# Transposing DMAs of one plane of a block, or of both planes together, in place of four small ones, in a two-layer decoder trunk

## The chip, the cores and the metric

The kernel runs on one core of one Trainium2 chip. The metric is the device time of one execution in microseconds. The time before is 2111.49 us, the median of three runs (2111.09 to 2111.51).

## The reference

Two pre-norm residual layers over 256 rows of 2048 columns in float32. The first mixes with sliding-window attention and an mLSTM, the second with forgetting attention; each is followed by a SwiGLU FFN with 5632 hidden columns.

```python
def swiglu(xn, w_gate, w_up, w_down):
    return (jax.nn.silu(xn @ w_gate) * (xn @ w_up)) @ w_down

    h = x
    for layer in range(DEPTH):
        j = layer // 2
        xn = rms_norm(h, norm_mix[layer])
        if layer % 2 == 0:
            mix = swa_mlstm_mixer(xn, w_in_even[j], w_out_even[j], ...)
        else:
            mix = forgetting_attention_mixer(xn, w_in_odd[j], fox_b_f[j], w_out_odd[j])
        h = h + mix.astype(h.dtype)
        h = h + swiglu(rms_norm(h, norm_ffn[layer]), w_gate[layer], w_up[layer], w_down[layer])
    return rms_norm(h, norm_final)
```

## The kernel before

**Matmuls.** Every float32 operand is split into a high and a low part: ScalarE (ACT) casts to `hi`, VectorE (DVE) subtracts to `lo`, and TensorE (PE) makes three products per tile (`hi` by `hi`, `lo` by `hi`, `hi` by `lo`; lines 184 to 186 and 394 to 396). The activations are kept transposed, 16 column blocks of 128 partitions by 256 rows, in `xh`/`xl` (the normed stream) and `mh`/`ml` (the mixer's outputs, later the FFN's hidden columns). The weights are streamed: `load_raw` (line 112) issues one DMA of 512 KB on SyncE's queue (SP) for each 256 rows by 512 columns, `split_chunk` (lines 156, 157) splits it. Four `raw` buffers and six `hi`/`lo` pairs lie between the load and the matmul; where `pair_group` multiplies two blocks by a scheme with fewer products (`prod`, `ht`/`lt`, `sx`, `sd`), DVE and ACT have more to do per weight block.

**Turned blocks.** A result of a matmul has rows on partitions; as the left operand of the next it must be transposed. For most blocks of 512 columns (both halves of 128 rows, that is 256 by 512 float32) this is done by DMA, which transposes 16-bit elements only. So a block is cut into two *planes*, the low and the high 16 bits of each number:

1. ACT copies each plane into `flat` (128 partitions; two planes of 1024 elements: `t` 0 and 1, 512 columns each): line 235 for the stream `h`, line 587 for FFN blocks.
2. SP issues one transposing DMA for each plane and each half `t`, four in all, each of 128 by 512 elements, into `turned` (lines 241 and 589).
3. `join`: ACT copies each plane of `turned` back to its place among the 16-bit halves of `ct` (lines 246 and 594; one copy reads 1024 elements in a row and writes every second one), and the result is scaled and split into `xh`/`xl` (lines 251, 252) or split into `mh`/`ml` (lines 271, 272); DVE also makes sums of it (`sums_of`, lines 224 to 227) for the scheme with fewer products.

`turn_scaled` does this for the residual stream behind an output projection or the last part of a FFN, 12 blocks in all (four after the first mixer, four between the layers, four after the second mixer). For even `n` its `flat` lies in the tile `c` and its planes are two tiles `turned`; for odd `n` three tiles named `turn` hold the flat planes, the turned planes and the joined block. The FFN's loop turns 20 more blocks of hidden columns (ten per layer), always through `c` and `turned`; the last hidden block of a part goes through TensorE instead.

**Order.** The program is written in the order of the code, and `issue_after` ties a turn's start to a weight load and a join to a cast; within that, a planner sets the order of the instructions on every engine from its own estimate of their times. SP takes its queue in order: a DMA behind another is issued when that one has been, and a DMA whose buffer or source is not ready holds what is behind it. ACT and DVE take their work in order too.

Of the kernel before, what the change touches and what calls it, by code (L numbers as in the profile page):

```python
# [10 lines left out]
U16 = mybir.dt.uint16  # L11
# [6 lines left out]
P = 128  # L18
D = 2048
S = 256  # L20
NT = S // P
KT = D // P
FF = 5632
NB = 512
# [35 lines left out]
def trunk(  # L60
# [20 lines left out]
    nc = tc.nc  # L81
# [137 lines left out]
    def sums_of(room, sh, sl, copies, full=None):  # L219
# [7 lines left out]
        nc.vector.tensor_tensor(out=s[:, 3, :], in0=full[:, 1, 0, :], in1=s[:, 1, :], op=ALU.subtract)  # L227
        split_plain(sh, sl, s)

    def turn_scaled(room, idx, n, extra=None):  # L230

        hu = h[:, :, n * NB : (n + 1) * NB].bitcast(U16).rearrange("p t (n b) -> p t n b", b=2)
        flat, turned, ct = room.turn_tiles(n % 2)
        for b in range(2):
            nc.scalar.copy(flat[:, b, :, :], hu[:, :, :, b])

        def start():
            with tc.issue_after(load[0].ins):
                for b in range(2):
                    for t in range(NT):  # L240
                        nc.sync.dma_start_transpose(turned[b][:, :, t, :], flat[:, b, t, :])

        def join():
            cb = ct.bitcast(U16).rearrange("p (n b) -> p n b", b=2)
            for b in range(2):
                nc.scalar.copy(cb[:, :, b], turned[b].rearrange("p k t q -> p (k t q)"))
            cols = ct.rearrange("p (k q) -> p k q", k=4)
            for i in range(4):
                k = 4 * n + i
                g = gT[:, idx * KT + k : idx * KT + k + 1]  # L250
                nc.scalar.mul(xh[:, k, :], cols[:, i, :], g)
                nc.vector.scalar_tensor_tensor(
                    out=xl[:, k, :], in0=cols[:, i, :], scalar=g, in1=xh[:, k, :].bitcast(F32), op0=ALU.mult, op1=ALU.subtract
                )
            for half in range(2):
                pair = 2 * n + half
                if extra is None or pair not in mixed_of(ORDER):
                    continue
                m = mixed_of(ORDER).index(pair)

                def copies(full, half=half, pair=pair):
                    for i in range(2):
                        g = gT[:, idx * KT + 2 * pair + i : idx * KT + 2 * pair + i + 1]
# [137 lines left out]
    class Room:  # L401
# [23 lines left out]
            return self.pool.tile(shape, F32, tag="tmp", name=name, bufs=2)  # L425

        def turn_tiles(self, odd):
            shape = [P, 4, NT, P]
            if odd:
                a, b, ct = (self.pool.tile([P, 2 * NB], F32, tag="raw", name="turn", bufs=self.raws) for _ in range(3))  # L430
                flat = a.bitcast(U16).rearrange("p (b t n) -> p b t n", b=2, t=NT)
                turned = [
                    b.bitcast(U16)[:, i * 2 * NB : (i + 1) * 2 * NB].rearrange("p (k t q) -> p k t q", k=4, t=NT)
                    for i in range(2)
                ]
                return flat, turned, ct
            c = self.c()
            flat = (
                c[:, 2:4, :].bitcast(U16).rearrange("p a n -> p (a n)").rearrange("p (b t n) -> p b t n", b=2, t=NT)
            )  # L440
            turned = [self.pool.tile(shape, U16, tag="tmp", name="turned", bufs=2) for _ in range(2)]
            return flat, turned, c[:, 0:2, :].rearrange("p a n -> p (a n)")

    class Inside(Room):
# [93 lines left out]
    def ffn(layer, fp, room, pending, sx, sd, key, idx_next=None, key_next=None, finish=None, then=None):  # L538
# [6 lines left out]
        for g0, g1 in zip(PARTS, PARTS[1:]):  # L545
# [5 lines left out]
            for g in range(g0, g1):  # L551
                par = (g1 - 1 - g) % 2
                plain, c = pair_group(
                    room, par, x_of, sums_x, [(w_gate[layer], g * NB), (w_up[layer], g * NB)], ORDER, todo
                )
                todo = []
                for m in range(2):
                    for t in range(NT):
                        o = c[:, 2 * m + t, :]
                        nc.vector.tensor_tensor(out=o, in0=plain[m][t], in1=o, op=ALU.add)  # L560
                for t in range(NT):
                    nc.scalar.activation(c[:, t, :], c[:, t, :], AF.Silu, scale=r[:, t : t + 1])
                for t in range(NT):
                    nc.vector.scalar_tensor_tensor(
                        out=c[:, t, :], in0=c[:, 2 + t, :], scalar=r[:, t : t + 1], in1=c[:, t, :], op0=ALU.mult, op1=ALU.mult
                    )
                if g == g1 - 1 and nk < 16:
                    for half in range(2):
                        pt = bank(par, "pf").rearrange("p (i q) -> p i q", i=2)
                        for i in range(2):  # L570
                            cs = (2 * half + i) * P
                            for t in range(NT):
                                nc.tensor.transpose(pt[:, i, t * P : (t + 1) * P], c[:, t, cs : cs + P], ident)
                        pair = 2 * (g - g0) + half
                        k = 2 * pair
                        split_plain(mh[:, k : k + 2, :], ml[:, k : k + 2, :], pt)
                        if pair in mixed_of(order):
                            j = mixed_of(order).index(pair)
                            sums_of(
                                room, sd[0][:, j, :, :], sd[1][:, j, :, :], lambda full, pt=pt: nc.scalar.copy(full, pt)  # L580
                            )
                    continue
                cu = c.bitcast(U16).rearrange("p a (n b) -> p a n b", b=2)
                flat = c[:, 2:4, :].bitcast(U16).rearrange("p a n -> p (a n)").rearrange("p (b t n) -> p b t n", b=2, t=NT)
                turned = [fp.tile([P, 4, NT, P], U16, tag="tmp", name="turned") for _ in range(2)]
                for b in range(2):
                    nc.scalar.copy(flat[:, b, :, :], cu[:, 0:2, :, b])
                    for t in range(NT):
                        nc.sync.dma_start_transpose(turned[b][:, :, t, :], flat[:, b, t, :])
                def join(c=c, turned=turned, g=g, g0=g0, order=order):  # L590
                    ct = c[:, 0:2, :].rearrange("p a n -> p (a n)")
                    cb = ct.bitcast(U16).rearrange("p (n b) -> p n b", b=2)
                    for b in range(2):
                        nc.scalar.copy(cb[:, :, b], turned[b].rearrange("p k t q -> p (k t q)"))
# [15 lines left out]

                todo = [(MID if g < g1 - 1 else MID_DOWN, join)]
# [17 lines left out]
            for n0 in (0, 2):  # L629
                if end and idx_next is None and n0 == 2:  # L630
# [68 lines left out]
    with tc.tile_pool(name="ev", bufs=1) as ev:  # L699
# [156 lines left out]
        with tc.tile_pool(name="mp", bufs=1) as mp:  # L856
# [31 lines left out]
            plain, c = pair_group(room, 0, x_of, sums_m, [(wi, OFF_QM), (wi, OFF_KM)], QK_ORDER)  # L888
# [79 lines left out]
            plain, c = pair_group(room, 0, x_of, sums_m, [(wi, OFF_VM), (wi, OFF_VM + NB)], QK_ORDER)  # L968
# [51 lines left out]
    with tc.tile_pool(name="od", bufs=1) as od:  # L1020
# [62 lines left out]
        for i in range(4):  # L1083
# [141 lines left out]
```

## Time and profile before

| | |
|---|---|
| median of three runs | 2111.49 us |
| the profiled execution | 2111.74 us |
| its span (first to last instruction) | 2110.0 us |
| mean granted TensorE clock | 0.998 |
| PE, DVE, ACT busy | 99%, 86%, 63% of the span |
| transposing DMAs | 128: 80 on line 589, 48 on line 241 |
| weight and input loads on SP, 512 KB | 4.4 to 4.9 us from issue to landing in the median, by matrix |

PE, DVE, ACT and POOL are the engines' busy times; PEld is TensorE's load of the stationary operand, which overlaps PE. SPq stands for SP's issuing instructions: their durations are the time that SP is held by one issue, not the transfer. In the waits, `A <- B: us, times, longest` says that A was idle until B was done. A row of windows gives, for a stretch, the busy time of each engine and in brackets the number of instructions, then the granted clock, the share of DMA time and the GB/s.

### The profile page before, as it was taken

What the parts mean: (1) busy time and instruction counts of PE and PEld (TensorE: products, weight loads), DVE (VectorE), ACT (ScalarE), POOL (GpSimd) and SP (SyncE); (2) the same over time, 40 slices, a digit from 0 to 9 for tenths busy, and PEclk for the clock granted to TensorE, in tenths of its full rate; (3) what the DMA queues carried; (4) which work ended last, traced back from release to release, by engine and by line L of the source; (5) the groups of instructions that cost most, each with busy time, mean ns of one, the idle gap of its engine ahead of it and who ended that gap; (6) DMA issues with size and microseconds to landing.
All of it is one profiled execution on the core that took longest, in us unless ns stands there. A gap on an engine that the chain in (4) does not pass through costs nothing.

```text
span 2110.0 us, 26911 instructions
## 1 busy us (share of the span) xinstructions
PE 2088.3 (99%) x9558; PEld 1729.4 (82%) x9558; DVE 1817.7 (86%) x2402; ACT 1326.3 (63%) x1685; POOL 51.3 (2%) x74
## 2 busy tenths in 40 slices
PE   8999999999999999999999999999999999999998
PEld 6878888888888888888888888887888888888886
DVE  6688757998999999998788878669989999998985
ACT  6575568665577656667765555586755677556763
POOL 2101000000000000000000000000000000000000
PEclk9999999999999999999999999999999999999999
DMA  9446677756677657766685655576756667657763
GB/s 321 120 140 191 218 191 218 251 189 201 191 222 232 210 196 223 210 209 170 197 244 185 186 177 173 167 219 227 237 173 222 221 210 207 219 192 213 228 198 139
DMA packets 285111, 429.35 MB, mean 203 GB/s; under 512 B 82688, under 2 KB 90928, under 8 KB 284976
## 3 DMA queue, kind: packets, MB, share of 16 engines
q1 hardware_dynamic: 283088, 421.79, 64.2%
q0 software_dynamic: 1744, 5.81, 0.9%
q8 instruction: 75, 1.23, 0.2%
q14 instruction: 60, 0.49, 0.1%
q10 hardware_dynamic: 144, 0.03, 0.0%
HBM read 408.67 MB, written 2.11 MB: 195 GB/s over the span
## 4 chain that ended last, share of the span: by engine, by line
PE 82%; DVE 8%; DMA 4%; ACT 3%; issue 2%; SPq 0%; POOLq 0%; POOL 0%; ACTq 0%; DVEq 0%
PE acc L395 17%; PE acc L396 17%; PE acc L394 17%; PE prod L395 4%; PE prod L394 4%; PE prod L396 4%; PE acc L186 4%; PE acc L185 4%; PE acc L184 4%; DVE lo L157 3%; DMA raw<-in_w_up_dram 1%; ACT hi L156 1%; DVE lt L272 1%; PE vacc L186 1%; PE vacc L184 1%
## 5 line engine op out<-in xcount | busy, mean ns | idle before, releaser
L156 ACT CAST hi<-raw 128x1024 fp32r<-128x1024 f32 (+1 forms) x664 | 675.3, 1030 | 431.5 <-PE acc L396 201.1
L157 DVE TENSOR_TENSOR lo<-raw,hi 128x1024 fp32r<-128x1024 f32 (+1 forms) x664 | 786.7, 1199 | 137.6 <-ACT hi L156 135.5
L395 PE MATMUL acc<-lo,xh 128*128 128x512 f32 x1207 | 471.2, 390 | 1.8 <-DVE lo L157 1.8
L396 PE MATMUL acc<-hi,xl 128*128 128x512 f32 x1207 | 467.2, 390 | 0.0
L394 PE MATMUL acc<-hi,xh 128*128 128x512 f32 x1207 | 464.8, 391 | 0.5 <-DVE c L533 0.4
L395 PEld LDWEIGHTS acc<-lo,xh 128*128 128x128 f32 x1207 | 226.8, 188 | 50.5 <-DVE lo L157 4.0
L394 PEld LDWEIGHTS acc<-hi,xh 128*128 128x128 f32 x1207 | 226.6, 188 | 49.3 <-DVE c L533 1.2
L396 PEld LDWEIGHTS acc<-hi,xl 128*128 128x128 f32 x1207 | 226.8, 188 | 46.8
L395 PE MATMUL acc<-lo,mh 128*128 128x512 f32 x444 | 173.1, 390 | 0.0
L396 PE MATMUL acc<-hi,ml 128*128 128x512 f32 x444 | 170.6, 390 | 0.0
L394 PE MATMUL acc<-hi,mh 128*128 128x512 f32 x444 | 169.7, 390 | 0.2 <-ACT hi L156 0.2
L271 ACT CAST ht<-raw 128x1024 fp32r<-128x1024 f32 x94 | 98.7, 1050 | 63.7 <-PE acc L396 29.6
L271 ACT CAST hi<-raw 128x512 fp32r<-128x512 f32 (+1 forms) x115 | 72.4, 630 | 86.1 <-PE acc L396 67.3
L271 ACT CAST ht<-t 128x1024 fp32r<-128x1024 f32 x94 | 98.8, 1051 | 43.8 <-PE prod L396 36.5
L184 PE MATMUL acc<-hi,mh 128*128 128x512 f32 x320 | 126.3, 396 | 0.0
L272 DVE TENSOR_TENSOR lt<-raw,ht 128x1024 fp32r<-128x1024 f32 x94 | 114.9, 1223 | 12.4 <-ACT ht L271 12.2
L185 PE MATMUL acc<-lo,mh 128*128 128x512 f32 x320 | 125.2, 391 | 0.0
L186 PE MATMUL acc<-hi,ml 128*128 128x512 f32 x320 | 124.9, 392 | 0.0
L272 DVE TENSOR_TENSOR lt<-t,ht 128x1024 fp32r<-128x1024 f32 x94 | 114.8, 1221 | 0.3 <-ACT ht L271 0.2
L394 PEld LDWEIGHTS acc<-hi,mh 128*128 128x128 f32 x444 | 83.4, 188 | 17.9 <-ACT hi L156 0.7
L395 PEld LDWEIGHTS acc<-lo,mh 128*128 128x128 f32 x444 | 83.4, 188 | 17.8 <-DVE lo L157 0.5
L396 PEld LDWEIGHTS acc<-hi,ml 128*128 128x128 f32 x444 | 83.4, 188 | 17.0
(387 smaller groups left out, 3554.1 us busy)
## 6 DMA issues: line engine op xcount, KB each, us to landing
raw<-in_w_gate_dram SPq DMA_DIRECT2D x176, 512.0 KB, 4.6
raw<-in_w_up_dram SPq DMA_DIRECT2D x176, 512.0 KB, 4.7
raw<-in_w_down_dram SPq DMA_DIRECT2D x176, 512.0 KB, 4.9
raw<-in_w_in_odd_dram SPq DMA_DIRECT2D x88, 512.0 KB, 4.4
raw<-in_w_in_even_dram SPq DMA_DIRECT2D x64, 512.0 KB, 4.6
raw<-in_w_out_even_dram SPq DMA_DIRECT2D x32, 512.0 KB, 4.4
raw<-in_w_out_odd_dram SPq DMA_DIRECT2D x32, 512.0 KB, 4.7
raw<-in_w_in_odd_dram SPq DMA_DIRECT2D x8, 272.0 KB, 5.0
```

What stands on the lines that cost most here:

```text
L156: latest[0] = nc.scalar.copy(hi[:, :, 0:n], raw[:, :, 0:n])
L157: nc.vector.tensor_tensor(out=lo[:, :, 0:n], in0=raw[:, :, 0:n], in1=hi[:, :, 0:n].bitcast(F32), op=ALU.subtract)
L184: nc.tensor.matmul(o, ah[:, ts], hi, start=(k == 0), stop=False)
L185: nc.tensor.matmul(o, ah[:, ts], lo, start=False, stop=False)
L186: nc.tensor.matmul(o, al[:, ts], hi, start=False, stop=(k == k_all - 1))
L271: nc.scalar.copy(dst_h, src)
L272: nc.vector.tensor_tensor(out=dst_l, in0=src, in1=dst_h.bitcast(F32), op=ALU.subtract)
L394: nc.tensor.matmul(o, ah, hi, start=start, stop=False)
L395: nc.tensor.matmul(o, ah, lo, start=False, stop=False)
L396: nc.tensor.matmul(o, al, hi, start=False, stop=stop)
```

## The change

The planes of `flat` are no longer addressed by half, and a plane of 128 by 1024 elements is transposed by one DMA into `turned` with 8 blocks of 128. Where both planes of the target lie in one tile (the `turn` tiles of odd `n`), one DMA transposes both, 128 by 2048 elements into 16 blocks. In the result the half `t` is now the outer index and the column block `k` the inner one, so the join's copy reads its 1024 elements as 8 runs of 128 in another order (`k`, then `t`). In the FFN loop both flat copies now stand ahead of the DMAs in the code. Counts: 20 FFN blocks and 6 scaled ones with two DMAs each, 6 scaled ones with one: 58 in place of 128. Bytes, copies and matmuls stay.

```diff
+    def turn_planes(turned, flat):
+        if len(turned) == 1:
+            nc.sync.dma_start_transpose(turned[0], flat.rearrange("p b n -> p (b n)"))
+            return
+        for b in range(2):
+            nc.sync.dma_start_transpose(turned[b], flat[:, b, :])
+
+    def join_planes(cb, turned):
+        for b in range(2):
+            one = turned[b] if len(turned) == 2 else turned[0][:, 8 * b : 8 * b + 8, :]
+            nc.scalar.copy(
+                cb[:, :, b].rearrange("p (k t q) -> p k t q", k=4, t=NT), one.rearrange("p (t k) q -> p k t q", t=NT)
+            )
+
     def turn_scaled(room, idx, n, extra=None):
...
         for b in range(2):
-            nc.scalar.copy(flat[:, b, :, :], hu[:, :, :, b])
+            nc.scalar.copy(flat[:, b, :].rearrange("p (t n) -> p t n", t=NT), hu[:, :, :, b])
 
         def start():
             with tc.issue_after(load[0].ins):
-                for b in range(2):
-                    for t in range(NT):
-                        nc.sync.dma_start_transpose(turned[b][:, :, t, :], flat[:, b, t, :])
+                turn_planes(turned, flat)
 
         def join():
             cb = ct.bitcast(U16).rearrange("p (n b) -> p n b", b=2)
-            for b in range(2):
-                nc.scalar.copy(cb[:, :, b], turned[b].rearrange("p k t q -> p (k t q)"))
+            join_planes(cb, turned)
...
         def turn_tiles(self, odd):
-            shape = [P, 4, NT, P]
             if odd:
...
-                flat = a.bitcast(U16).rearrange("p (b t n) -> p b t n", b=2, t=NT)
-                turned = [
-                    b.bitcast(U16)[:, i * 2 * NB : (i + 1) * 2 * NB].rearrange("p (k t q) -> p k t q", k=4, t=NT)
-                    for i in range(2)
-                ]
+                flat = a.bitcast(U16).rearrange("p (b n) -> p b n", b=2)
+                turned = [b.bitcast(U16).rearrange("p (i q) -> p i q", q=P)]
                 return flat, turned, ct
...
-            turned = [self.pool.tile(shape, U16, tag="tmp", name="turned", bufs=2) for _ in range(2)]
+            turned = [self.pool.tile([P, 8, P], U16, tag="tmp", name="turned", bufs=2) for _ in range(2)]
...
-                turned = [fp.tile([P, 4, NT, P], U16, tag="tmp", name="turned") for _ in range(2)]
+                turned = [fp.tile([P, 8, P], U16, tag="tmp", name="turned") for _ in range(2)]
                 for b in range(2):
-                    nc.scalar.copy(flat[:, b, :, :], cu[:, 0:2, :, b])
-                    for t in range(NT):
-                        nc.sync.dma_start_transpose(turned[b][:, :, t, :], flat[:, b, t, :])
+                    nc.scalar.copy(flat[:, b, :].rearrange("p (t n) -> p t n", t=NT), cu[:, 0:2, :, b])
+                turn_planes(turned, flat)
...
-                    for b in range(2):
-                        nc.scalar.copy(cb[:, :, b], turned[b].rearrange("p k t q -> p (k t q)"))
+                    join_planes(cb, turned)
```

The planner sets the order anew. On SP, at the joint of the two layers, where the last blocks of the first layer's stream are turned between the loads of its FFN's last weights and those of the second layer (`w_in_odd`), the queue before was:

```order
L241 DMA_TRANSPOSE turned<-c 128x4x128 x4
L241 DMA_TRANSPOSE turn<-turn 128x4x128 x4
L112 DMA raw<-in_w_down_dram 128x2x512 x6
L112 DMA raw<-in_w_in_odd_dram 128x2x512 x4
L112 DMA raw<-in_w_in_odd_dram 128x2x272 x4
L112 DMA raw<-in_w_in_odd_dram 128x2x512 x2
L241 DMA_TRANSPOSE turned<-c 128x4x128 x4
L241 DMA_TRANSPOSE turn<-turn 128x4x128 x4
L112 DMA raw<-in_w_in_odd_dram 128x2x512 x2
```

and is now, with lines 235 and 232 for the DMA of one plane and of both:

```order
L235 DMA_TRANSPOSE turned<-c 128x8x128 x2
L232 DMA_TRANSPOSE turn<-turn 128x16x128
L112 DMA raw<-in_w_down_dram 128x2x512 x6
L112 DMA raw<-in_w_in_odd_dram 128x2x512 x4
L112 DMA raw<-in_w_in_odd_dram 128x2x272 x4
L112 DMA raw<-in_w_in_odd_dram 128x2x512 x2
L235 DMA_TRANSPOSE turned<-c 128x8x128 x2
L112 DMA raw<-in_w_in_odd_dram 128x2x512 x2
L232 DMA_TRANSPOSE turn<-turn 128x16x128
L112 DMA raw<-in_w_in_odd_dram 128x2x272 x4
```

Two weight loads moved ahead of the last block's transpose; elsewhere on SP the places of the transposes among the loads are the same, or differ by one or two loads.

On ACT, in a FFN block of the first layer (`c<-c` are the flat copies, `c<-turned` the joins, `hi` and `ht` casts of weights, `mh` the cast of the joined block), the rows before were:

```order
L587 COPY c<-c 128x1024 x2
L156 COPY hi<-raw 128x1024 x2
L271 COPY ht<-t_6325 128x1024
L594 COPY c<-turned 128x1024
L271 COPY ht<-raw 128x1024
L594 COPY c<-turned 128x1024
L156 COPY hi<-raw 128x1024
L271 COPY mh<-c 128x1024
```

and are now:

```order
L592 COPY c<-c 128x1024 x2
L156 COPY hi<-raw 128x1024 x2
L282 COPY ht<-t_6303 128x1024
L240 COPY c<-turned 128x1024 x2
L282 COPY ht<-raw 128x1024
L282 COPY mh<-c 128x1024
L156 COPY hi<-raw 128x1024
```

The two joins stand together and the block's cast one weight cast earlier. In 14 of the 20 FFN blocks the two joins stood together before as well.

More of the change, by code (lines that the diff above doesn't have):

```diff
@@ L427, in turn_tiles @@
         def turn_tiles(self, odd):
-            shape = [P, 4, NT, P]
             if odd:
                 a, b, ct = (self.pool.tile([P, 2 * NB], F32, tag="raw", name="turn", bufs=self.raws) for _ in range(3))
-                flat = a.bitcast(U16).rearrange("p (b t n) -> p b t n", b=2, t=NT)
-                turned = [
-                    b.bitcast(U16)[:, i * 2 * NB : (i + 1) * 2 * NB].rearrange("p (k t q) -> p k t q", k=4, t=NT)
-                    for i in range(2)
-                ]
+                flat = a.bitcast(U16).rearrange("p (b n) -> p b n", b=2)
+                turned = [b.bitcast(U16).rearrange("p (i q) -> p i q", q=P)]
                 return flat, turned, ct
             c = self.c()
-            flat = (
-                c[:, 2:4, :].bitcast(U16).rearrange("p a n -> p (a n)").rearrange("p (b t n) -> p b t n", b=2, t=NT)
-            )
-            turned = [self.pool.tile(shape, U16, tag="tmp", name="turned", bufs=2) for _ in range(2)]
+            flat = c[:, 2:4, :].bitcast(U16).rearrange("p a n -> p (a n)").rearrange("p (b n) -> p b n", b=2)
+            turned = [self.pool.tile([P, 8, P], U16, tag="tmp", name="turned", bufs=2) for _ in range(2)]
             return flat, turned, c[:, 0:2, :].rearrange("p a n -> p (a n)")
@@ L583, in ffn @@
                 cu = c.bitcast(U16).rearrange("p a (n b) -> p a n b", b=2)
-                flat = c[:, 2:4, :].bitcast(U16).rearrange("p a n -> p (a n)").rearrange("p (b t n) -> p b t n", b=2, t=NT)
-                turned = [fp.tile([P, 4, NT, P], U16, tag="tmp", name="turned") for _ in range(2)]
+                flat = c[:, 2:4, :].bitcast(U16).rearrange("p a n -> p (a n)").rearrange("p (b n) -> p b n", b=2)
+                turned = [fp.tile([P, 8, P], U16, tag="tmp", name="turned") for _ in range(2)]
                 for b in range(2):
-                    nc.scalar.copy(flat[:, b, :, :], cu[:, 0:2, :, b])
-                    for t in range(NT):
-                        nc.sync.dma_start_transpose(turned[b][:, :, t, :], flat[:, b, t, :])
+                    nc.scalar.copy(flat[:, b, :].rearrange("p (t n) -> p t n", t=NT), cu[:, 0:2, :, b])
+                turn_planes(turned, flat)
                 def join(c=c, turned=turned, g=g, g0=g0, order=order):
```

## The prediction

> **What bounds the kernel now.** I read the page's busy table first, then the windows, to see where TensorE is not fed, and last the waits and the chain in those places.
>
> ```profile
> span 2110.0 us, 26911 instructions
> PE 2088.3 (99%) x9558; PEld 1729.4 (82%) x9558; DVE 1817.7 (86%) x2402; ACT 1326.3 (63%) x1685; POOL 51.3 (2%) x74
> ```
>
> TensorE is the bound: idle for 2110.0 - 2088.3 = 21.7 us. No change to transposing DMAs removes a matmul, so the gain is limited by idle time. Whole windows say where it lies (columns: window, PE, PEld, DVE, ACT and POOL busy with instruction counts, granted clock, DMA share, GB/s).
>
> ```profile
> 0.00:20.00 20.00, 12.63 (x43) 8.96 (x44) 11.11 (x21) 12.94 (x23) 3.51 (x14) 1.00 0.90 289
> 450.00:500.00 50.00, 49.45 (x222) 40.63 (x222) 44.46 (x59) 28.56 (x35) 0.00 (x0) 1.00 0.66 226
> 550.00:600.00 50.00, 50.00 (x222) 41.42 (x222) 45.98 (x55) 33.68 (x36) 0.00 (x0) 1.00 0.73 222
> 2100.00:2110.00 10.00, 1.44 (x7) 0.86 (x5) 3.04 (x6) 2.87 (x4) 0.55 (x1) 0.81 0.53 210
> ```
>
> The first 20 us hold 7.4 us of the idle time (the first loads) and the last 10 us hold 8.6 (the final norm and the store). Neither has a transposing DMA. That leaves 5.7 us. An ordinary FFN window, 550 to 600, has none at all, although a block is turned in it (the first of these two, SP's timeline):
>
> ```profile
> 585.59 5.13 SPq L589 DMA_TRANSPOSE turned<-c  x4
> 590.83 1.89 SPq L112 DMA_DIRECT2D raw<-in_w_gate_dram  x1
> ...
> 624.67 5.19 SPq L589 DMA_TRANSPOSE turned<-c  x4
> ```
>
> Narrow windows at the places near turned blocks where PE is idle:
>
> ```profile
> 1016.00:1020.00 4.00, 3.76 (x17) 2.80 (x16) 4.00 (x8) 4.00 (x7) 0.00 (x0) 1.00 0.55 157
> 1044.00:1048.00 4.00, 3.06 (x18) 2.56 (x18) 2.38 (x5) 4.00 (x7) 0.00 (x0) 1.00 0.59 108
> 1050.00:1054.00 4.00, 3.88 (x18) 2.75 (x17) 2.54 (x5) 3.63 (x7) 0.00 (x0) 1.00 0.62 213
> 1064.00:1068.00 4.00, 3.29 (x16) 2.44 (x16) 4.00 (x9) 3.09 (x5) 0.00 (x0) 1.00 0.77 219
> 1076.00:1080.00 4.00, 3.84 (x17) 2.88 (x16) 3.57 (x7) 3.56 (x6) 0.00 (x0) 1.00 0.45 131
> 380.00:384.00 4.00, 3.60 (x16) 2.47 (x15) 4.00 (x5) 1.05 (x1) 0.00 (x0) 1.00 0.81 260
> 1428.00:1430.00 2.00, 1.94 (x9) 1.29 (x8) 0.92 (x1) 1.05 (x1) 0.00 (x0) 1.00 1.04 381
> 1452.00:1456.00 4.00, 3.04 (x12) 1.88 (x11) 4.00 (x5) 1.05 (x1) 0.00 (x0) 1.00 0.83 268
> sum 30.00, PE 26.40 PEld 19.07 DVE 25.41 ACT 21.43 POOL 0.00; mean PE 3.30 PEld 2.38 DVE 3.18 ACT 2.68 POOL 0.00
> ```
>
> Together 30.00 - 26.40 = 3.6 us: 2.2 at the joint of the two layers (1016 to 1080) and 1.4 in the two FFN starts. PE's busy time hides a part of each stall, since matmuls overlap. The weight loads show the rest: undisturbed they are busy 41.42 of 50 us, so 30 us should hold 24.85 and hold 19.07; the 5.78 us that are missing are 7.0 us of time. The loss lies between 3.6 and 7.0; I take the middle, **5.3 us: 3.2 at the joint, 2.1 in the FFN starts.** All of it is 0.25% of the time.
>
> Who is waited for there (waits of the weight loads, 1000 to 1090), and the chain just behind SP's transposes:
>
> ```profile
> PEld acc L395 <- DVE lo L157: 2.0, 3, 1.1
> PEld vacc L184 <- ACT xh L251: 1.4, 2, 1.2
> PEld acc L394 <- ACT hi L156: 1.2, 2, 0.7
> ...
> 1043.44 0.72 SPq L241
> ...
> 1044.21 1.27 SPq L241
> ...
> 1045.58 4.72 DMA raw<-in_w_in_odd_dram
> ```
>
> `hi` and `lo` are split from a weight block that came late, and it came late because SP was still issuing transposes. `xh` waits for the turned block itself.
>
> **The change part by part.** *The issues on SP.* There are 32 turned blocks of four DMAs each:
>
> ```profile
> L589 SPq DMA_TRANSPOSE turned<-c x80: 1194/1253/2379, 401.0 to 2032.8; - x80
> ...
> L241 SPq DMA_TRANSPOSE turned<-c x24: 1194/1258/1452, 292.9 to 1401.7; - x24
> L241 SPq DMA_TRANSPOSE turn<-turn x24: 1195/1238/2286, 299.7 to 1417.1; - x24
> ...
> DMA to landing us min/median/max: 2.4/2.6/5.4
> ...
> 990.04 5.12 SPq L241 DMA_TRANSPOSE turned<-c  x4
> 995.26 6.16 SPq L241 DMA_TRANSPOSE turn<-turn  x4
> 1001.53 3.35 SPq L112 DMA_DIRECT2D raw<-in_w_down_dram  x6
> ...
> 1035.11 5.12 SPq L241 DMA_TRANSPOSE turned<-c  x4
> 1040.33 5.15 SPq L241 DMA_TRANSPOSE turn<-turn  x4
> 1045.58 2.06 SPq L112 DMA_DIRECT2D raw<-in_w_in_odd_dram  x4
> ```
>
> 128 instructions become 58: the 20 FFN blocks and 6 of the 12 scaled blocks have two each, the other 6 one. What SP pays for an instruction twice or four times as large no row shows. From below it is the 1.25 us of the small one; from above 2.5 and 5.0 us, in proportion. The small ones cost 1194 ns at least and 1253 in the median, almost regardless of what the queue carries, which looks like a fixed price; so I take 1.25 us for a plane, and 2.4 us for both planes, near the longest hold seen (2379). A block then takes 2.5 or 2.4 us of SP in place of 5.1, and the loads behind it go some 2.6 us earlier; where two blocks follow each other at the joint, 5.5 us earlier (10.4 for the two from 1035.11 on, less 4.9). In the FFN blocks that is worth nothing: the cover is the blocks already loaded and split, and PE stands at 50.00 of 50. If that cover were gone, 20 blocks at 2.6 us would be 52 us, which is why nothing shows only as long as DVE keeps up.
>
> *Landing.* The last quarter of a block now lands 3 x 1.25 + 2.6 = 6.4 us after its first issue. With two planes issued 1.25 us apart it is 1.25 + 2.6, and up to 1.3 us more for twice the bytes (as its issue would take more): 3.9 to 5.2. With one DMA it is 2.6 plus up to 3 x 1.25: no later than now. The one thing that comes later is the first plane of an odd block, which had landed after 1.25 + 2.6 = 3.9 us.
>
> *Copies.* The join reads runs of 128 in another order, the counts and sizes are the same:
>
> ```profile
> L235 ACT COPY turn<-h 128x1024 uint16<-128x1024 uint16 x12 | 11.9, 1041 | 0.1
> L594 ACT COPY c<-turned 128x1024 uint16<-128x1024 uint16 x40 | 52.8, 1358 | 6.2 <-DMA turned<-c 6.0
> L246 ACT COPY c<-turned 128x1024 uint16<-128x1024 uint16 x12 | 16.2, 1358 | 0.8 <-DMA turned<-c 0.8
> ```
>
> A copy of this size that writes runs takes 1041 ns, one that writes every second half-word 1358; the join writes as before and only its reads are cut into runs, so I take 0. At worst it pays such a difference again: 64 copies by 0.3 us = 19 us of ACT, which is idle for 37% of the span. The single DMA of an odd block needs both flat copies first (2.0 us in place of 1.0), but SP now reaches it with time in hand.
>
> *What comes back.* At the joint the late loads (1016, 1052, 1064, 1076: 0.24 + 0.12 + 0.71 + 0.16 = 1.2 us of the 2.2) go: 1.8 of the 3.2. At 1044 `xh` stands behind a row of copies on ACT (4.00 of 4.00 busy), which the shorter SP time moves only in part: half of the other 1.4, 0.7. In the FFN starts DVE is 4.00 of 4.00 busy when PE waits; that backlog began with late loads,
>
> ```profile
> 343.54 2.42 DMA turn<-turn
> ...
> 351.30 6.83 DMA raw<-in_w_up_dram
> ```
>
> but DVE's own work has its share: half of 2.1, 1.05. Sum: 1.8 + 0.7 + 1.05 = 3.55 us.
>
> *The order.* The planner moves DVE and ACT work along with the joins. A stall made by order alone is what the window 450 to 500 shows: 0.55 us. Below nothing (a lucky order) and above some 6 us (the second rival) are its ends; I take one such stall in each layer, 1.1 us.
>
> Net: 3.55 - 1.1 = 2.45 us less. The profiled execution took 2111.74 us, its span 2110.0 and 1.74 around it; the median of the runs shown is 2111.49, 0.25 lower. 2111.49 - 2.45 = **2109.0 us**.
>
> **The rivals.** *SP pays by size.* A plane holds SP for 2.5 us, both for 5.0; loads go out as now, and nothing is gained. For it: the price of one instruction covers whatever SP does per piece of it. Against it: the floor of 1194 ns does not move. Time: 2111.5, or 2112.6 with the 1.1 us of order. The Trainium skill has such a rule (DMA: Bandwidth & Descriptors, "Why a DMA increments its semaphore by 16 and not by 1"): its table of DMA transposes inside SBUF sets a single push for the whole transpose against one push per tile in earlier generations. By it the instruction's price would follow its size, and this rival's 2111.5 would be the time; no run of before can show it, since all its transposes have one size.
>
> *The joins wait and the splits behind them are late.* Place: the FFN joins on ACT. Both copies now stand next to each other ahead of the `hi` casts, and ACT takes its work in order; if a plane lands later than the planner thinks, casts, DVE's `lo` and PE follow. Four of the 40 copies waited 6.0 us already, 1.5 each. Price: FFN blocks are 39 us apart (585.59 and 624.67), and DVE, 46 of 50 us busy in the window quoted, has some 2 to 3 us of slack in a block. It decides from a wait of about 2.5 us per join; at 0.3 us beyond it, 20 blocks give 6 us: 2117.5. Against it: by the sums above the planes land earlier, and most FFN joins had their two copies together before.
>
> *All of it goes.* Loads and turned blocks come early enough everywhere and the order costs nothing: 2111.5 - 5.3 = 2106.2.
>
> **How the numbers follow.** The forecast has 0.40, payment by size 0.20, the slower joins 0.22, all of it 0.18. What can be told from no change is about 0.2%, 4.2 us: faster is below 2107.3, slower above 2115.7. Faster takes nearly all of the last rival (0.17). Slower takes the joins and a worse order under another name: 0.24. The rest, the forecast and payment by size, is within: 0.59. The forecast's own range is 2107 to 2111. For 8 in 10 it reaches down to the last rival with a little more (2105.8) and up to the near part of the slower one: **2105.8 to 2116.0**.
>
> **What would show it.** On SP a plane's DMA at about 1.25 us and a pair's at 2 to 2.5, and the load behind a group at the joint 5 us after the group's start, not 10.4; 2.5 and 5.0 would be payment by size. PE's idle time at 1016 to 1080 should fall from 2.2 us to under 1, and at the FFN starts from 1.4 to about 0.7. ACT's wait for `turned` should not grow beyond 6.8 us; if it does, and DVE's `lo` is waited for within ordinary FFN windows, the joins decided. I am wrong in the step and not only in size if PE's idle time moves at places where no block is turned.

## The result, and the profile after

| | before | after |
|---|---|---|
| median, 13 runs each | 2111.72 us | 2107.03 us |
| lowest and highest | 2108.24 to 2114.35 | 2105.24 to 2108.51 |
| profiled execution, its span | 2111.74, 2110.0 | 2107.07, 2105.4 |

The ratio is 0.9977, 95% interval 0.9969 to 0.9986: 4.7 us less (3.0 to 6.5), where 2.45 were forecast. The ratio is just over the 0.2% that the prediction took as the least that can be told from no change; the near end of its interval, 0.14%, is not. Single executions of one kernel lie 1.5 to 3.5 us to either side of the median, so verdicts below rest on ratios over many runs, and two single traces tell places, not tenths.

The page of after, its span and busy times:

```profile
span 2105.4 us, 26803 instructions
PE 2085.8 (99%) x9558; PEld 1729.8 (82%) x9558; DVE 1819.2 (86%) x2402; ACT 1324.4 (63%) x1685; POOL 50.3 (2%) x74
```

PE is idle for 19.6 us in place of 21.7, and 2.5 us less "busy": in a stall the matmuls that overlap stretch, as the prediction said, so the idle time alone shows less than half of the 4.6 us that the span lost. The windows of after at the eight places of the prediction, and one more (columns: window, PE, PEld, DVE, ACT and POOL busy with instruction counts, granted clock, DMA share, GB/s):

```profile
1016.00:1020.00 4.00, 4.00 (x19) 3.34 (x18) 4.00 (x7) 2.33 (x3) 0.00 (x0) 1.00 0.62 143
1044.00:1048.00 4.00, 3.04 (x17) 2.16 (x16) 4.00 (x7) 4.00 (x8) 0.00 (x0) 1.00 0.81 224
1050.00:1054.00 4.00, 4.00 (x24) 3.56 (x24) 4.00 (x10) 2.91 (x7) 0.00 (x0) 1.00 0.59 157
1064.00:1068.00 4.00, 4.00 (x19) 3.27 (x19) 4.00 (x8) 3.00 (x6) 0.00 (x0) 1.00 0.73 215
1076.00:1080.00 4.00, 4.00 (x24) 3.40 (x23) 4.00 (x8) 2.10 (x3) 0.00 (x0) 1.00 0.95 303
380.00:384.00 4.00, 4.00 (x19) 3.32 (x18) 3.97 (x6) 0.57 (x2) 0.00 (x0) 1.00 0.83 296
1428.00:1430.00 2.00, 2.00 (x11) 1.65 (x10) 2.00 (x3) 1.84 (x3) 0.00 (x0) 1.00 0.13 19
1452.00:1456.00 4.00, 4.00 (x19) 3.30 (x18) 2.94 (x5) 2.88 (x3) 0.00 (x0) 1.00 0.26 98
424.00:428.00 4.00, 3.05 (x14) 2.21 (x13) 3.57 (x6) 0.62 (x1) 0.00 (x0) 1.00 0.02 9
```

Seven of the eight stalls are gone; of 3.6 us of idle time 0.96 are left, all at 1044. The last row is a new stall of 0.95 us in a FFN block of the first layer, where before had none:

```profile
424.00:428.00 4.00, 4.00 (x19) 3.22 (x18) 4.00 (x7) 1.00 (x2) 0.00 (x0) 1.00 0.01 4
```

Who is waited for in after, by the weight loads: first all rows above 0.2 us from 1000 to 1090, then the one from 420 to 432.

```profile
PEld vacc L186 <- DVE xl L263: 0.9, 1, 0.9
PEld vacc L184 <- ACT xh L262: 0.8, 1, 0.8
...
PEld acc L405 <- DVE u L537: 1.4, 1, 1.4
```

`lo` and `hi`, the splits of late weights, are no longer in the list from 1000 to 1090; `xh` and `xl`, which are made from the turned block, still are. What stands ahead of `xh` on ACT, its timeline in after tells (start, duration, count):

```profile
1039.10 2.58 ACT L240 COPY c<-turned 128x1024 uint16<-128x1024 uint16 x2
...
1042.17 2.94 ACT L156 CAST hi<-raw 128x1024 fp32r<-128x1024 f32 x3
1045.01 1.71 ACT L262 ACTIVATE xh<-c,gT 128x256 fp32r<-128x256 f32 x4
```

The block is turned and joined at 1041.68 (1039.10 + 2.58), but three casts of weights go first. At 424 PE waits for `u`, which DVE makes; ahead of it DVE had itself waited for a weight load, longer than before (1.55 us in its row there):

```profile
424.43 0.69 DVE L511 TENSOR_TENSOR t<-raw 128x512 f32<-128x512 f32 x1 [2.77 <-DMA raw<-in_w_up_dram]
```

So this stall, too, begins with a late load.

SP's prices, by tile (min/median/max ns), the landing of each, and the join (busy us, mean ns, idle time before it):

```profile
L235 SPq DMA_TRANSPOSE turned<-c x52: 1237/1280/3474, 293.0 to 2025.7; - x52
DMA to landing us min/median/max: 3.1/3.9/6.4
L232 SPq DMA_TRANSPOSE turn<-turn x6: 1765/2404/5387, 301.8 to 1410.1; - x6
DMA to landing us min/median/max: 4.2/4.6/7.4
...
L240 ACT COPY c<-turned 128x1024 uint16<-128x1024 uint16 x52 | 67.4, 1353 | 0.5 <-DMA turned<-c 0.5
```

A plane costs SP what a quarter of a block did. ACT waits 0.5 us in all for `turned` and as much for `turn`, in place of 6.8. And SP at the joint:

```profile
1033.65 2.66 SPq L235 DMA_TRANSPOSE turned<-c  x2
1036.42 1.05 SPq L112 DMA_DIRECT2D raw<-in_w_in_odd_dram  x2
1037.66 5.39 SPq L232 DMA_TRANSPOSE turn<-turn  x1
1043.14 12.09 SPq L112 DMA_DIRECT2D raw<-in_w_in_odd_dram  x10
```

Two loads now go out at 1036.42, between the blocks; the single DMA of both planes, issued behind them, holds SP for 5.39 us.

### The profile page after: what moved, and what is told of

Its sections match the earlier page's. It is cut to its first block, busy times and chain, and to the rows that moved or that the text cites. A ratio compares the mean times of both kernels' runs of the same rounds, so it can differ in the third digit from the quotient of the medians.

```text
span 2105.4 us, 26803 instructions
## 1 busy us (share of the span) xinstructions
PE 2085.8 (99%) x9558; PEld 1729.8 (82%) x9558; DVE 1819.2 (86%) x2402; ACT 1324.4 (63%) x1685; POOL 50.3 (2%) x74
## 3 DMA queue, kind: packets, MB, share of 16 engines
q8 instruction: 75, 1.23, 0.2%
## 4 chain that ended last, share of the span: by engine, by line
PE 91%; DVE 4%; DMA 2%; issue 1%; ACT 1%; SPq 0%; POOLq 0%; POOL 0%; DVEq 0%; ACTq 0%
PE acc L405 19%; PE acc L406 19%; PE acc L407 19%; PE acc L186 5%; PE acc L185 5%; PE acc L184 5%; PE prod L405 5%; PE prod L406 5%; PE prod L407 5%; DVE lo L157 2%; DMA raw<-in_w_up_dram 1%; PE vacc L186 1%; PE vacc L184 1%; PE vacc L185 1%; PE ptm L294 1%
## 5 line engine op out<-in xcount | busy, mean ns | idle before, releaser
L282 ACT CAST ht<-t 128x1024 fp32r<-128x1024 f32 x94 | 98.9, 1052 | 54.3 <-PE prod L407 46.9
```

The source lines that it names most:

```text
L282: nc.scalar.copy(dst_h, src)
```

## The experiments

Three theories stood against each other. **SP's time:** loads behind a block are issued earlier. **Landing:** the turned blocks are there earlier. **Order:** the planner, which sees other transfers, puts the work in a luckier order. All kernels were timed beside runs of before on the same chip; the ratio is to those.

**Which blocks.** `e1_scaled_only` goes back to four small DMAs in the 20 FFN blocks, `e2_ffn_only` in the 12 scaled ones, `e3_four_small_new_layout` in all, with the new layout and joins kept.

```diff
+    def turn_quarters(turned, flat):
+        for b in range(2):
+            whole = turned[b] if len(turned) == 2 else turned[0][:, 8 * b : 8 * b + 8, :]
+            for t in range(NT):
+                nc.sync.dma_start_transpose(whole[:, 4 * t : 4 * t + 4, :], flat[:, b, t * NB : (t + 1) * NB])
...
-                turn_planes(turned, flat)
+                turn_quarters(turned, flat)
```

> Wide DMAs only for the 12 scaled blocks (before the FFNs and between the layers); the 20 FFN blocks go back to four DMAs of 128 by 512 each. Theory A (SP's time: the loads behind a group of transposes go out earlier) and theory B (the turned blocks land earlier) both say that the whole gain is made by the scaled blocks: at the joint of the layers about 3.3 us and at the two FFN starts 2.7, as in the changed kernel, and that the stall of 1.2 us that the changed kernel has at 425 to 433 us belongs to the FFN blocks and is gone: 4.7 to 6 us less than before. Theory C (the planner's new order happens to be better, whatever the DMAs cost) gives no reason for either: anything from 0 to 5 us less.

> The other half alone: wide DMAs for the 20 FFN blocks, four small ones for the 12 scaled blocks. Theories A and B: no gain, since no stall of before lies behind an FFN block, and perhaps the stall of 1.2 us at 425 to 433 us: 0 to 1.5 us more than before. Theory C: a part of the gain, 1 to 4 us less.

> The changed kernel with its layout (half outer, column block inner), its join copies and its order of flat copies and DMAs in the code, but every transpose cut into four of 128 by 512 again. Theories A and B: as before, within 1.5 us, and SP held about 5.1 us by each block. Theory C, or a gain from the layout: 2 to 5 us less, as the changed kernel.

| | median us | ratio | interval |
|---|---|---|---|
| `e1_scaled_only` | 2109.0 | 0.9991 | 0.9982 to 1.0000 |
| `e2_ffn_only` | 2110.6 | 0.9998 | 0.9989 to 1.0007 |
| `e3_four_small_new_layout` | 2110.42 | 0.9997 | 0.9988 to 1.0005 |

The layout and the joins are worth nothing, as the prediction had it: PE, DVE and ACT have the very order of before in `e3_four_small_new_layout`. The FFN blocks alone bring nothing that shows. The scaled blocks alone brought 2 us (between 0 and 3.8 by the interval) and not the 4.7 that were expected, a miss. In the trace of `e1_scaled_only` both FFN starts are full and the stall at 424 is gone, as expected (it is gone in `e2_ffn_only` as well, so it belongs to neither kind of block alone). But at the joint its weight loads waited for

```profile
PEld vacc L184 <- ACT xh L268: 2.2, 1, 2.2
```

in place of the late loads: as in the change, three casts of weights (2.94 us) stand between the joins and `xh` on ACT. Whether this stall is all that is missing is not shown.

**One DMA for both planes, or two.** `e4_planes_no_pair` gives odd blocks two DMAs as well. No trace of it is used here.

```diff
-            nc.sync.dma_start_transpose(turned[0], flat.rearrange("p b n -> p (b n)"))
-            return
+            turned = [turned[0][:, 8 * b : 8 * b + 8, :] for b in range(2)]
```

> One DMA for each plane everywhere, none for both planes together. Theory A: SP is held 2.5 us by the two planes of an odd block where the single DMA held it 1.8 to 5.4, so the time is that of the changed kernel within 1 us. Theory B: the first plane of an odd block lands about 1 us earlier than both together, the second about as the single DMA: the same or up to 1 us less. If the larger the DMA the better, 1 us more.

2106.91 us, ratio 0.9979 (0.9969 to 0.9988): the same as the change. The form for both planes has no part in the gain that shows.

**The order alone, and the DMAs alone.** The planner's estimate of a transposing DMA's time was changed so that each form of DMA ran under the order of the other: in `w1_wide_old_order` the DMAs of the change under before's order (258 places of PE differ, the first at 968 us, ahead of the joint), in `s1_small_new_order` the four small DMAs, by `turn_quarters`, under the order of the change (410 places differ, from 1014 us on, at the joint and behind it). Neither order is held fully, above all not at the joint. The estimate of the first, then of the second:

```diff
+TRN2Spec.DMA_TRANSPOSE_NS_PER_TILE = 28.0
+TRN2Spec.DMA_TRANSPOSE_TILES_LEFT_AT_SEQUENCER_RELEASE = 27
...
+TRN2Spec.DMA_TRANSPOSE_SEQUENCER_RELEASE_LEAD_NS = 700
+TRN2Spec.DMA_TRANSPOSE_NS_PER_TILE = 13.0
```

> The changed kernel's DMAs (planes and pairs) under the order of before: the planner's own estimate of a transposing DMA is raised (time per piece 28 in place of 14 ns, SP held longer), so that it plans about what it planned for four small ones. SP's order of loads and transposes is that of before, PE's differs from it at 258 of 9387 places, none of them before the last part of the first layer's FFN and none in the second FFN start. What the chip does per DMA is that of the changed kernel. Theory A (SP's time) and theory B (landing): the gain stays, 4 to 5 us less than before. Theory C (the planner's new order): the gain is gone, within 1.5 us of before, and the stalls at 381 and 1452 us are back.

> The reverse: four small DMAs a block under the order of the changed kernel, by an estimate that lets SP go earlier (release lead 700 in place of 125 ns, 13 ns per piece). PE's order is that of the changed kernel except at 410 of 9387 places, all at and behind the joint of the layers; both FFN starts are the same. Theories A and B: no gain, 2110 to 2113, more if the order counts on data that are not there. Theory C: the gain stays, 3 to 5 us less than before, with PE's stall at 381 us gone.

`w1_wide_old_order`: 2107.48 us, ratio 0.9982 (0.9973 to 0.9990). `s1_small_new_order`: 2118.29 us, ratio 1.0034 (1.0021 to 1.0047). The gain of the whole stays with the DMAs and not with the order; under nearly the new order the small DMAs even cost 7 us. The windows of `s1_small_new_order` show where, and its waits from 1000 to 1090 (of PE's weight loads) and from 1005 to 1062 (of ACT) for whom:

```profile
1016.00:1018.00 2.00, 0.87 (x4) 0.61 (x4) 2.00 (x4) 2.00 (x4) 0.00 (x0) 1.00 0.01 3
1048.00:1050.00 2.00, 0.73 (x6) 0.51 (x5) 1.39 (x3) 2.00 (x3) 0.69 (x1) 1.00 0.49 99
...
PEld vacc L188 <- ACT xh L272: 2.6, 2, 2.0
PEld acc L188 <- ACT hi L160: 1.5, 1, 1.5
...
ACT hi L160 <- DMA raw<-in_w_in_odd_dram: 7.0, 6, 2.1
```

Stalls of more than 1.1 us stand at the joint. PE waits there for `xh` and for splits of weights, and ACT, which makes `xh` and casts the weights in one row, waits for late loads.

In `w1_wide_old_order` the load behind the two blocks of the joint is issued 6.1 us after the group's start (1034.72 to 1040.81) in place of 10.5, and the stalls at 1044 and 1064 are both gone: there `xh` follows right on the joins, with no casts between. So the stall that the change keeps at 1044 goes with its order.

At one place, though, the order does what the DMAs do. The stall at 381, at the start of the first FFN, is gone in `w1_wide_old_order`, but also in `s1_small_new_order` with its small DMAs, and it is still there in `v2_planes_no_424_stall` below, which has a DMA for each plane under before's order. `s1_small_new_order`, then `v2_planes_no_424_stall`:

```profile
380.00:384.00 4.00, 4.00 (x19) 3.30 (x18) 3.97 (x6) 0.57 (x2) 0.00 (x0) 1.00 0.77 261
...
380.00:384.00 4.00, 3.39 (x14) 2.18 (x13) 4.00 (x5) 1.05 (x1) 0.00 (x0) 1.00 0.82 267
```

**SP's time or landing.** The wide DMAs do both. To take SP's time back and leave the landing, something had to hold SP behind each block. A first try, `e5_sp_held`, issued seven tiny copies from the flat planes to DRAM.

```diff
+        with tc.issue_after(end.ins):
+            for _ in range(7):
+                spare.append(spare.pop(0))
+                nc.sync.dma_start(spare[-1], flat[:, 1, 0:8])
```

> The changed kernel with seven tiny copies to DRAM (2 KB each) on SP behind each block's transposes, at 0.37 us or more of issue each: SP is held about as long as before by each block, 2.5 us of transposes and 2.6 of copies, while the blocks land as in the changed kernel. The planner knows of the copies and orders anew, so PE's order is that of neither kernel. Theory A: the gain is gone, within 1.5 us of before. Theory B: 3 to 5 us less than before. Theory C: nothing follows.

2206.99 us, ratio 1.0450 (1.0435 to 1.0464): some 96 us more, as no theory had it, and not a test of them. The planner set another order, and the copies made a wait of their own, since they read the tile that ACT writes next (5.4 us of the 96; the rest is not traced to a place):

```profile
ACT turn L246 <- DMA spare<-turn: 5.4, 1, 5.4
```

The next try put instructions into the finished program, behind the last DMA of each block of `w1_wide_old_order`, so that no other engine's order can move. `h1_wide_old_order_sp_held` used register moves, the two others waits on a semaphore that is already met.

```diff
+    hold = nc.alloc_semaphore("hold", num=140)
+    now, half = [nc.sync.sem_clear(hold).ins, nc.sync.sem_inc(hold, 1).ins], 0
+    for one in body.instructions:
+        now.append(one)
+        if type(one).__name__ != "InstDmaTransposeAnt":
+            continue
+        half += 1 if "@turned_" in str(one) else 2
+        if half == 2:
+            half = 0
+            for _ in range(count):
+                now.append(nc.sync.wait_ge(hold, 1).ins)
```

> The DMAs of the change under the order of before (as in w1_wide_old_order, 2107.5), and behind the last DMA of each block 40 register moves on SP, put into the finished program, so that no instruction of another engine changes its place. What a move takes no run has shown; the trace will tell it by the start of the next load. Where the 40 hold SP for about 2.6 us, what the four small DMAs held it longer: if the gain is SP's time (loads issued earlier), 2110.5 to 2111.5, as before, and in proportion where they hold it shorter or longer. If it is that the turned blocks land earlier, which the moves leave as it is: 2107.5 whatever they take.

> As h1_wide_old_order_sp_held, whose register moves are not in its trace (26784 instructions, as without them); in their place 60 waits on a semaphore that is already met, behind the last DMA of each block. In the trace of w1_wide_old_order such a wait of SP at 1040.77 us has its successor 0.04 us later, so 60 should hold SP for some 2.4 us. If the gain is SP's time: 2110.5 to 2111.5, as before. If it is that the turned blocks land earlier: 2107.5.

> As h2_wide_old_order_sp_waits with 120 waits. There 30 of each 60 are in the trace and held SP for 1.8 us (the next load 1.92 us behind the transposes in place of 0.09), 70% of the 2.6 us that the small DMAs held it longer; so here 3.7 us, 1.4 times that. If the gain is SP's time, the 0.0018 of w1_wide_old_order goes and more: 0.0018 in 2.6 us is 0.0007 for each us, so a ratio of 0.9982 + 0.0026 = 1.0008, 2113. If it is that the turned blocks land earlier: 0.9982, 2107.5 to 2108, as without waits. Half of each: 0.9995.

| | SP held longer, per block | median us | ratio | interval |
|---|---|---|---|---|
| `w1_wide_old_order` | 0 | 2107.48 | 0.9982 | 0.9973 to 0.9990 |
| `h1_wide_old_order_sp_held` | 0 | 2108.11 | 0.9981 | 0.9972 to 0.9990 |
| `h2_wide_old_order_sp_waits` | 1.8 us | 2109.43 | 0.9990 | 0.9981 to 0.9999 |
| `h3_wide_old_order_sp_waits_twice` | 3.7 us | 2125.31 | 1.0070 | 1.0058 to 1.0082 |

The moves left no instruction in the trace, so the first of them repeats `w1_wide_old_order` and no more. The waits held SP: in `w1_wide_old_order` a FFN block and the load behind it stand in SP's timeline as

```profile
585.38 2.60 SPq L239 DMA_TRANSPOSE turned<-c  x2
588.07 0.72 SPq L116 DMA_DIRECT2D raw<-in_w_gate_dram  x1
```

and in `h2_wide_old_order_sp_waits` as

```profile
584.99 2.60 SPq L239 DMA_TRANSPOSE turned<-c  x2
589.52 0.38 SPq L116 DMA_DIRECT2D raw<-in_w_gate_dram  x1
```

0.09 us between the two became 1.93. With 1.8 us (70% of the 2.6 that the change saves in a block) half of the gain is gone in the medians, though the intervals overlap. The trace of `h2_wide_old_order_sp_waits`, of the fastest of its eleven runs, shows no place that lost: PE is full in all eight windows of the prediction and in those quoted next. With 3.7 us the gain is gone and 14 us with it. The windows of `h3_wide_old_order_sp_waits_twice` show where:

```profile
340.00:362.00 22.00, 19.59 (x85) 15.35 (x84) 17.93 (x33) 17.23 (x28) 0.69 (x1) 1.00 0.75 238
380.00:440.00 60.00, 58.08 (x254) 46.99 (x253) 56.77 (x71) 37.79 (x42) 0.00 (x0) 1.00 0.64 207
550.00:600.00 50.00, 50.00 (x223) 41.40 (x222) 47.37 (x58) 31.52 (x35) 0.00 (x0) 1.00 0.63 197
1050.00:1062.00 12.00, 9.14 (x44) 7.03 (x43) 5.19 (x9) 9.01 (x14) 0.45 (x1) 1.00 0.65 175
1432.00:1440.00 8.00, 5.46 (x24) 3.85 (x23) 6.16 (x12) 5.53 (x9) 0.00 (x0) 1.00 0.85 285
```

In `w1_wide_old_order` PE is 22.00, 60.00, 50.00, 12.00 and 8.00 busy there. A longer hold of SP is paid for at the start of the first FFN, at the joint and at the start of the second FFN, and not in ordinary FFN blocks (PE is busy throughout from 550 to 1000 us). These are the three places where the change gained. At the joint the hold also sends off the second block's transposes 2.7 us later behind the first's, but PE does not wait for their landing: the joins run without a wait, and then ACT stands still for a weight, ahead of `xh`.

```profile
1058.64 1.04 ACT L160 CAST hi<-raw 128x1024 fp32r<-128x1024 f32 x1 [2.96 <-DMA raw<-in_w_in_odd_dram]
```

So at the joint SP's time alone, by late loads, can make such stalls. That before's stalls at the FFN starts were made the same way is not shown, and SP's timeline speaks against it. Behind the last block turned ahead of the first FFN, in before and then in `w1_wide_old_order`:

```profile
340.94 5.12 SPq L241 DMA_TRANSPOSE turn<-turn  x4
348.43 1.95 SPq L112 DMA_DIRECT2D raw<-in_w_gate_dram  x2
...
342.18 1.83 SPq L236 DMA_TRANSPOSE turn<-turn  x1
348.72 1.75 SPq L116 DMA_DIRECT2D raw<-in_w_gate_dram  x2
```

In before SP was done with the four DMAs at 346.06 and issued the next load only at 348.43, since that load waited for its buffer (SP's waits there are for DVE's `lo` and ACT's copies). With one DMA it went out no sooner: in both kernels 8.6 us after ACT began the block's flat copies, and in `h3_wide_old_order_sp_waits_twice` too. Ahead of the second FFN it is 9.3 us in before and 8.6 in `w1_wide_old_order`, but 8.6 also in `e3_four_small_new_layout` with small DMAs. What took the stalls at the FFN starts away is open; an earlier landing is not excluded. Time that SP has to spare ahead of a load would also explain why 1.8 us of holding cost little and 3.7 much; that is not shown.

**The price by itself.** `p2_transposes_alone` leaves out the whole computation and only loads and transposes.

> Leaves out the whole computation; SP issues transposing DMAs of 128x512, 128x1024 and 128x2048 elements: first six of each, each behind the landing of the one before; then eight of each one behind the other into eight tiles; then, three times, four loads of 512 KB with four small, two of a plane or one of both planes behind them, and two loads behind those. If the price of an issue is fixed up to a plane and the rest is a full queue: alone 1.2, 1.25 and 1.8 us; one behind the other the 128x2048 grows to above 2.4 us, since the queue is full of its predecessors; behind four loads the pair is held 4 to 5.5 us. If SP pays for the size itself: 1.25, 2.5 and 5.0 us in all three places.

Each behind the landing of the one before (by tile, min/median/max ns):

```profile
L103 SPq DMA_TRANSPOSE quarter<-flat x6: 1189/1190/1300, 6.2 to 18.5; - x6
...
L103 SPq DMA_TRANSPOSE plane<-flat x6: 1232/1232/1309, 19.7 to 35.1; - x6
...
L103 SPq DMA_TRANSPOSE pair<-flat x6: 1317/1800/1961, 36.4 to 58.0; - x6
```

Then SP's timeline (start, us from the first to the end of the last, count): eight in a row, and a whole block behind four loads.

```profile
62.84 10.35 SPq L103 DMA_TRANSPOSE quarter<-flat  x8
74.91 10.86 SPq L103 DMA_TRANSPOSE plane<-flat  x8
88.17 19.54 SPq L103 DMA_TRANSPOSE pair<-flat  x8
...
110.52 6.64 SPq L103 DMA_TRANSPOSE quarter<-flat  x4
...
126.59 6.33 SPq L103 DMA_TRANSPOSE plane<-flat  x2
...
142.28 6.52 SPq L103 DMA_TRANSPOSE pair<-flat  x1
```

Eight planes take SP 5% longer than eight quarters, so twice the elements are nearly free; eight pairs take 2.44 us each, which is more than one costs alone. Behind four loads a block takes 6.3 to 6.9 us in whatever form, over three rounds of each. I read this as SP being held by the loads ahead, so that the number of instructions no longer counts; no row names the cause. The 4 to 5.5 us expected there for a pair were too few.

**A better version.** `v2_planes_no_424_stall` has two DMAs for every block and an estimate that keeps before's order, without the new stall at 424.

```diff
+TRN2Spec.DMA_TRANSPOSE_NS_PER_TILE = 24.0
+TRN2Spec.DMA_TRANSPOSE_TILES_LEFT_AT_SEQUENCER_RELEASE = 16
```

> One DMA for each plane everywhere (none of both planes), and a planner's estimate of their times under which the order of before stays but for 212 places of TensorE. If the gain is SP's time and the stall at 424 us is the order's: 2106 to 2107, 0.5 to 1 us below the change. If the order of before has as many stalls elsewhere: 2107 to 2107.5, the same as the change.

2107.7 us, ratio 0.9984 (0.9975 to 0.9993): no faster than the change. The stall at 424 is gone, but the one at 381 is there (3.39 of 4.00 us, shown above), and one at 1044 (2.97 of 4.00). What a single stall costs cannot be told at this spread.

## Why the prediction came out as it did

The time lies inside the range and 2.0 us below the forecast. The mechanism held at the joint; at the FFN starts the gain came, but not by the way that the prediction gave for it, and several terms were off in size.

*SP's price: right.* 1.25 us was taken for a plane, 1.28 is the median, 1.23 it takes alone. 2.4 was taken for both planes and is the median, by chance: 1.8 alone, 5.39 behind two loads.

*Payment by size: refuted.* 1190, 1232 and 1800 ns for one, two and four times the elements. From a quarter to a plane, 42 ns for twice as much; only the pair costs more, and still not in proportion. By the Trainium skill's one push per tile in earlier generations (DMA: Bandwidth & Descriptors, "Why a DMA increments its semaphore by 16 and not by 1") the price would grow with the size; the rows show no such growth up to a plane, and they decide.

*"The load behind a group at the joint 5 us after the group's start, not 10.4": wrong.* It is 9.5 us, 1033.65 to 1043.14. What came earlier instead were the two loads that the planner moved between the blocks, out at 1036.42; the pair behind them then paid their backlog. That these two loads had moved was on record ahead of the prediction, in the order of SP, and my sum left it out. Where they stay behind the group, in `w1_wide_old_order`, it is 6.1 us, near the 5.

*Landing: right in size.* A block of two planes lands some 1.3 + 3.9 = 5.2 us after its first issue (3.9 to 5.2 was the estimate), a pair after 4.6 (up to 2.6 + 3 x 1.25 = 6.35 was the estimate).

*Copies at nothing: right.* The join takes 1353 ns in place of 1358.

*Late loads at the joint, 1.8 us: right.* The stalls at 1016, 1052, 1064 and 1076 are gone, and so are `hi` and `lo` from the waits there.

*Half of the stall at 1044, 0.7 us: wrong.* It was 0.94 us and is 0.96. The first block's planes did come back sooner, and both joins ended at 1041.68; but in the new order ACT casts three weights before it makes `xh`, and the time went there. I had written that the shorter SP time moves ACT's row of copies in part; it moved the copies and not the row's end. Under before's order the wide DMAs take the whole stall away (`w1_wide_old_order`, PE full from 1044 to 1048).

*The FFN starts, "half of 2.1, 1.05": undersized, and its cause is open.* All three stalls there went. I had seen DVE 4.00 of 4.00 busy and given it a share of its own. Late weights can make such stalls: when SP was held longer in `h3_wide_old_order_sp_waits_twice`, PE lost 2.4 us at 340 to 362, 1.9 at 380 to 440 and 2.5 at 1432 to 1440, with DVE's work as it was (1817.0 us busy in all, 1818.9 without the waits). In before, too, ACT waited 4.3 us for two `w_gate` loads from 335 to 384, and 0.5 in after. But the prediction laid the late loads to SP's transposes, and there the loads behind the last block waited for a buffer and go out no earlier now. And the new order with small DMAs has no stall at 381 either (`s1_small_new_order`).

*The order, 1.1 us: right in size, but not as made up.* One new stall came in place of two, at 424: 0.95 us of idle time, and 1.0 us of weight loads are missing (2.21 against 3.22). Under before's order the wide DMAs do not make it (`w1_wide_old_order`, PE full there). The new order also kept the stall at 1044, and by `s1_small_new_order` it can take the one at 381 away.

Put together with these sizes, 1.8 + 0 + 2.1 - 1.1 = 2.8 us. The ratio says 3.0 to 6.5. What is left is not put to a place: the loss of 5.3 itself was the middle of 3.6 and 7.0, and at its upper end (0.96 us of idle time left of 3.6, and 1.0 of 7.0 by the weight loads: 24.00 of 24.85 us in these windows) the eight places alone gave 6.0 us, 4.9 with the order's 1.1 taken off.

*The slower rival, joins that wait: refuted.* ACT's wait for `turned` fell from 6.8 to 0.5 us, and ordinary FFN windows stay full. *All of it goes: half right.* Seven of eight stalls went, but not the one at 1044, and a new one came at 424.

## What to carry to other kernels

A saving of queue time is worth what the few places pay where loads are late, not the count of instructions. Hold the queue longer on purpose and the trace shows the places that would pay for more; whether they paid before, look up in the queue's own timeline: a load that waits for a free buffer is not brought forward by a shorter issue ahead of it. An engine that is full in the window of a stall need not be its cause: look back for whether it is catching up on something late. And to split a change that moves a planner's order, run its DMAs under the old order and the old DMAs under the new, and compare place by place: a total can hide that either one is enough at one place.

## What was not expected of the hardware

A transposing DMA of 128x1024 elements costs SP nearly as little as one of 128x512 even eight in a row (10.86 against 10.35 us), while behind four loads of 512 KB a block takes 6.3 to 6.9 us in one, two or four DMAs: there the larger DMAs saved SP nothing. Of 60 waits on one met semaphore 30 are in the trace (960 instructions more for 32 blocks), some 0.06 us apart. And holding SP is far from linear: 1.8 us in a block cost 2 us of the run in the medians, 3.7 us cost 18.
